# First products that begin as the input arrives, shifted copies by DMA, and a third raw m-tile in the second block

## The chip, the cores and the metric

The kernel runs on one core of one Trainium2 chip. The metric is the device time of one execution in microseconds, from three runs of the kernel before. A core has a matrix engine (TensorE, PE), a vector engine (VectorE, DVE), an activation engine (ScalarE, ACT), GpSimd (POOL) and SyncE (SP); DMAs are issued from the queues of SP, ACT or POOL.

## What is computed

Two transformer blocks in a row, on one sequence of 512 tokens with 1024 channels, all in fp32. Cut to what the change touches:

```
h  = rmsnorm(x, norm_mix)                      # first block
q, kc, vc, ks, vs, kw, vw, gl = split(h @ w_in)
k_cmp = gelu(windows(kc) + pe_k) @ ck_w1 ...   # windows of 32 tokens, stride 16
v_cmp = gelu(windows(vc) + pe_v) @ cv_w1 ...
...                                            # attention, memory attention, conv ffn
x3 = residual;  x = rmsnorm(x3, final_norm)    # end of the first block
h  = rmsnorm(x, norm_g)                        # second block
u, v, za, ab, ab_gate, zb, g_a, g_b = split(h @ w_in_2 + b_in)
t  = ab * sigmoid(ab_gate)                     # then a causal convolution of 31 taps
y_a = gelu(u) * (ws @ layernorm(gelu(v)) + bs) * silu(za)
...                                            # merged, projected, added to x, gated once more
```

## The kernel before

Activations lie in SBUF with channels on the 128 partitions and the 512 tokens along the free dimension, so x is 8 tiles of 128x512. An fp32 operand is held as a high and a low part; `split` makes the high part on ACT and the low part on DVE. `mm` issues three matmuls (high by high, high by low, low by high), so that one output tile over 1024 input channels (`dense`) is 24 matmuls of 128x512. A weight piece of 128x1024 is fetched by SP into one of three slots `wr`, cast by ACT to a slot `wh`, and subtracted by DVE or POOL into a slot `wl` (`weight`; `share` says how many of four pieces go to POOL). The program order is not the order on the engines: a scheduler places instructions on each engine's queue by what they need and when it expects that, and each queue then runs strictly in its own order. All calls go through one wrapper, so every instruction has line 95, and the trace is read by the names of tiles: `x` tiles, products and temporaries are `a`, PSUM banks `ps`, small columns `s`.

**The beginning** (`nsa`, L289). The tiles of x are fetched alternately by SP and ACT, with the first weight in two halves between them. A loop (L304) scales and splits each x[k] and multiplies it at once into the first product `pk[0]`. The second product follows by `dense` (L598), then eight squares with their adds on POOL (`square_sum`), a third product, the sum over channels (`stat`, a matmul by ones), the fourth product, and a broadcast of the inverse norm `rb` over the partitions. Since rmsnorm's factor is per token, products are made from the unnormalised x and multiplied by `rb` after.

**Shifted copies** (`shifted`, L315). For the compressed keys and values each product tile of two groups is multiplied by `rb`, and then for each group ACT writes a tile whose upper 64 partitions hold the group's 64 channels and whose lower 64 hold the same one token later. `hidden` (L346) adds the position code to strided windows of these tiles (`wf`) and multiplies them by ck_w1 or cv_w1 in four quarters q. `keys` (L445) makes from one product two tiles with the same 64 channels in both halves of the partitions, in high and low part: two casts and two subtractions each. `token_gates` (L330) is a product of 16 matmuls and then a sum of its two halves (`fold`). It stands before `cmp_keys`, which takes a list of four jobs to be done between the quarters.

**The second block** (`block2`, L859). The norm of the first block and that of the second are folded into one factor. While it is worked out (`norms`, `norms_out`, L865 to L885), PE multiplies the raw operand: for the first RAW m-tiles the two products p4 and p3 are multiplied by the factor `R["b"]` after, and from m-tile RAW on the operand is the normalised and split one (`f` and `split` in `norms_out`). There DVE also makes the normalised first-block output in place, `t` times final_norm times `r3b`, which is read again only by the residual late in the block. The convolution is 31 taps a tile on DVE, each a SCALAR_TENSOR_TENSOR into a PSUM bank; `taps(n)` allows n more of them, with counts in TAPS for each stage: the m-loop, the two halves hf of v (four banks each, evicted by DVE, BATCH_NORM_STATS2 on each), the u loop, the mixing loop (`ya`), the loop of w_pa.

## Time and profile before

| what | value |
|---|---|
| time, median of 3 runs | 1464.67 us (1464.51 to 1468.86) |
| profiled execution | 1465.02 us, of which the span is 1463.2 us |
| mean granted TensorE clock | 0.993 of full speed |
| busy PE, DVE, ACT, POOL | 1424.6, 922.6, 659.7, 415.9 us |

The span runs from the first to the last instruction of the core; 1.8 us of the execution lie around it. In the timelines each row gives the start of a run of like instructions, its length, engine, operation, tiles (out<-in), form and count, and in brackets how long the engine had been idle before it and whom it waited for. Matmuls overlap, so the length of a pair is longer than their spacing.

### The profile page before, as it was taken

The page shows a single profiled execution, that of the slowest core. Times are in us where ns is not written, and L with a number is a line of the kernel's source. Part 1 is how long each engine was busy: PE and PEld are TensorE (multiplying, and loading weights), DVE is VectorE, ACT ScalarE, POOL GpSimd, SP SyncE. Part 2 cuts the span into 40 slices and gives each one's busy share as a digit, 9 for nine tenths or more (in the row PEclk, how much of TensorE's full clock was granted, in tenths as well). Part 3 has the DMA queues.
Part 4 walks back from the last instruction along what each step waited for, and adds up shares of the span by engine and source line. Part 5 has one row for each costly group of instructions (what it writes and reads, how often), then busy time and mean ns, then how long its engine had stood idle before and what let it go on. Part 6 is the DMA issues. An engine that isn't in the chain of part 4 may idle for free.

```text
span 1463.2 us, 18587 instructions
## 1 busy us (share of the span) xinstructions
PE 1424.6 (97%) x7106; PEld 1190.2 (81%) x7106; DVE 922.6 (63%) x1417; ACT 659.7 (45%) x1135; POOL 415.9 (28%) x347
## 2 busy tenths in 40 slices
PE   7999999999999999999999998999999999999997
PEld 5787878888888888888888886888887888888897
DVE  4858898886455455555643227999939774444464
ACT  4857768774344433332323333223244455423452
POOL 4023536542210221111111134443454440011223
PEclk9999999999999999999999999999999999999998
DMA  6242012114222233333323342332232322332331
GB/s 207 74 143 59 30 44 73 45 44 158 87 73 86 87 101 91 97 101 100 89 92 105 94 126 87 100 90 85 86 87 72 99 76 85 115 101 87 101 101 58
DMA packets 41384, 132.99 MB, mean 91 GB/s; under 512 B 5200, under 2 KB 7504, under 8 KB 41296
## 3 DMA queue, kind: packets, MB, share of 16 engines
q1 hardware_dynamic: 39568, 129.71, 29.4%
q10 hardware_dynamic: 1728, 2.10, 0.4%
q8 instruction: 56, 0.92, 0.3%
q14 instruction: 32, 0.26, 0.1%
HBM read 129.70 MB, written 2.10 MB: 90 GB/s over the span
## 4 chain that ended last, share of the span: by engine, by line
PE 87%; DVE 7%; ACT 2%; issue 1%; POOL 1%; DMA 1%; POOLq 0%; SPq 0%; ACTq 0%
PE ps L95 87%; DVE a L95 5%; ACT a L95 1%; POOL a L95 1%; DVE wl L95 1%; DVE ps L95 1%; ACT wh L95 1%; DMA a<-in_x_dram 1%; POOL wl L95 0%; DMA a<-in_mem_dram 0%; POOL s L95 0%; DVE s L95 0%; POOLq L1272 0%; SPq L95 0%; DVE wh L95 0%
## 5 line engine op out<-in xcount | busy, mean ns | idle before, releaser
L95 PE MATMUL ps<-a,wh 128*128 128x512 f32 (+1 forms) x3136 | 960.7, 388 | 6.8 <-ACT a L95 4.1
L95 PEld LDWEIGHTS ps<-a,wh 128*128 128x128 f32 x3136 | 584.5, 189 | 125.0 <-ACT a L95 5.3
L95 PE MATMUL ps<-a,wl 128*128 128x512 f32 (+1 forms) x1560 | 604.3, 387 | 2.5 <-POOL wl L95 2.4
L95 ACT CAST wh<-wr 128x1024 fp32r<-128x1024 f32 (+1 forms) x225 | 234.8, 1045 | 521.1 <-PE ps L95 319.3
L95 PEld LDWEIGHTS ps<-a,wl 128*128 128x128 f32 x1560 | 294.4, 189 | 61.8 <-POOL wl L95 3.9
L95 DVE TENSOR_TENSOR a<-ps,a 128x512 f32<-128x512 f32 (+5 forms) x284 | 169.9, 614 | 251.5 <-PE ps L95 197.0
L95 POOL TENSOR_TENSOR a<-a,a 128x512 f32<-128x512 f32 (+1 forms) x106 | 137.8, 1304 | 585.5 <-ACT a L95 470.0
L95 DVE TENSOR_TENSOR wl<-wr,wh 128x1024 fp32r<-128x1024 f32 x169 | 219.2, 1298 | 124.5 <-ACT wh L95 123.1
L95 PE MATMUL ps<-a,a 128*128 128x256 f32 (+4 forms) x1180 | 209.0, 321 | 8.3 <-ACT a L95 8.3
L95 POOL TENSOR_TENSOR wl<-wr,wh 128x1024 fp32r<-128x1024 f32 x56 | 134.1, 2395 | 176.6 <-ACT wh L95 167.8
L95 PEld LDWEIGHTS ps<-a,a 128*128 128x128 f32 x1180 | 165.2, 192 | 20.6 <-ACT a L95 10.7
L95 DVE SCALAR_TENSOR_TENSOR ps<-a,vecs,ps 128x483 f32<-128x483 f32 (+24 forms) x240 | 170.3, 735 | 4.5
L95 POOL TENSOR_TENSOR a<-a,s 128x512 f32<-128x512 f32 (+3 forms) x140 | 115.3, 852 | 184.4 <-DVE s L95 106.6
L95 DVE TENSOR_TENSOR a<-a,a 128x512 fp32r<-128x512 f32 (+3 forms) x172 | 120.8, 708 | 38.4 <-ACT a L95 23.9
L95 ACT CAST a<-a 128x512 fp32r<-128x512 f32 (+1 forms) x124 | 76.4, 622 | 77.9 <-DVE a L95 60.2
L95 ACT ACTIVATE a<-a 128x512 f32<-128x512 f32 (+1 forms) x114 | 61.6, 551 | 94.1 <-DVE a L95 93.9
L95 PE MATMUL ps<-wh,a 128*128 128x512 f32 (+1 forms) x320 | 93.6, 373 | 2.6 <-ACT wh L95 2.6
L95 ACT ACTIVATE a<-ps,s 128x256 f32<-128x256 f32 (+4 forms) x148 | 77.4, 528 | 27.3 <-DVE s L95 23.3
L95 DVE SCALAR_TENSOR_TENSOR a<-a,vecs,a 128x511 f32<-128x511 f32 (+3 forms) x92 | 73.3, 801 | 7.1 <-ACT a L95 6.2
L95 ACT CAST a<-ps 128x384 fp32r<-128x384 f32 (+2 forms) x132 | 62.9, 488 | 32.7 <-PE ps L95 27.4
L95 PEld LDWEIGHTS ps<-wh,a 128*128 128x128 f32 x320 | 58.8, 192 | 12.8 <-ACT wh L95 3.0
L95 DVE TENSOR_REDUCE s<-ps 128x1 f32<-128x128 f32 (+4 forms) x136 | 62.0, 490 | 5.1 <-PE ps L95 4.3
(80 smaller groups left out, 675.5 us busy)
## 6 DMA issues: line engine op xcount, KB each, us to landing
wr<-in_w_in_dram SPq DMA_DIRECT2D x56, 512.0 KB, 3.6
wr<-in_ffn_gate_dram SPq DMA_DIRECT2D x22, 512.0 KB, 3.6
wr<-in_ffn_val_dram SPq DMA_DIRECT2D x22, 512.0 KB, 3.5
wr<-in_ffn_d_dram SPq DMA_DIRECT2D x16, 512.0 KB, 3.5
wr<-in_nsa_w_in_dram SPq DMA_DIRECT2D x15, 512.0 KB, 3.6
wr<-in_ca_wk_dram SPq DMA_DIRECT2D x8, 512.0 KB, 3.6
wr<-in_ca_wv_dram SPq DMA_DIRECT2D x8, 512.0 KB, 3.6
wr<-in_nsa_w_out_dram SPq DMA_DIRECT2D x8, 512.0 KB, 3.6
```

Of the source, the lines that this page charges most:

```text
L95: return lambda *a, **k: f(*[_raw(x) for x in a], **{n: _raw(x) for n, x in k.items()})
```

## The change

The two first products begin together: two weights come in halves between the tiles of x, the loop multiplies each x[k] into both, and squares are taken inside it, added by DVE and POOL in turn. A small Square is issued before the first scaling. `shifted` multiplies by `rb` in half-height pieces straight into the two half tiles and fills the other halves by DMAs from POOL's queue, and `keys` copies halves in the same way. The gates' product moves into the list of jobs between the quarters of the compressed keys, as does its sum (`gates_turned`). In the second block RAW is 3, the normalised first-block output is a function `norm_x` that is called tile by tile, five times in the m-loop and three times in the first half of v, and the counts of taps are new: none for m-tiles 0 to 2, then 9 each, 5 in v, 6 with u, 4 in the mixing loop except its last turn, 10 with w_pa.

```diff
@@ -39,3 +39,3 @@
 
-TAPS = (4, 5, 5, 4, 10, 7)
+TAPS = (9, 5, 6, 4, 10)
 
@@ -45,3 +45,3 @@
 SHARE = (4, 0)
-RAW = 2
+RAW = 3
 DEBUG = False
@@ -290,11 +290,14 @@
         nc, I = self.nc, self.I
-        x, raws = [], []
-        w0 = self.wraw.tile([P, 1024], F32)
-        for k in range(KD):
-            x.append(self.a())
-            (nc.scalar if k % 2 else nc.sync).dma_start(x[k], I["x"][k])
-            if k in (0, 2):
-                nc.sync.dma_start(w0[:, 256 * k:256 * k + 512], I["nsa_w_in"][8][:, 256 * k:256 * k + 512])
-            if k in (4, 7):
-                raws.append(self.load(I["nsa_w_in"][9 + len(raws)]))
+        x, xs = [self.a() for _ in range(KD)], []
+        w0 = [self.wraw.tile([P, 1024], F32) for _ in range(2)]
+        for k in (0, 1, 3):
+            nc.scalar.dma_start(x[k], I["x"][k])
+        for c, ks in ((slice(0, S), (2, 4)), (slice(S, 2 * S), (5, 6, 7))):
+            for i in range(2):
+                nc.sync.dma_start(w0[i][:, c], I["nsa_w_in"][8 + i][:, c])
+            for k in ks:
+                nc.sync.dma_start(x[k], I["x"][k])
+        pre = self.sm(1)
+        nc.scalar.activation(pre, self.neghalf[:, 0:1], AF.Square)
+        raw = self.load(I["nsa_w_in"][10])
         nc.sync.dma_start(self.vecs[:, _FIRST:], I["vecs"][:, _FIRST:])
@@ -303,3 +306,13 @@
 
-        xs, w, pk = [], [], [self.ps()]
+        acc = []
+
+        def square(k):
+            sq = self.a()
+            nc.scalar.activation(sq, x[k], AF.Square)
+            if k < 2:
+                acc.append(sq)
+            else:
+                (nc.vector if k % 2 else nc.gpsimd).tensor_tensor(acc[k % 2], acc[k % 2], sq, op=ALU.add)
+
+        pk = [self.ps(), self.ps()]
         for k in range(KD):
@@ -307,5 +320,8 @@
             if k % 4 == 0:
-                w.append(self.split(w0[:, k * P:k * P + S]))
+                w = [self.split(t[:, k * P:k * P + S]) for t in w0]
             s = slice(k % 4 * P, k % 4 * P + P)
-            self.mm(pk[0], (w[k // 4][0][:, s], w[k // 4][1][:, s]), xs[k], k == 0, k == KD - 1)
+            for j in range(2):
+                self.mm(pk[j], (w[j][0][:, s], w[j][1][:, s]), xs[k], k == 0, k == KD - 1)
+            if k >= 2:
+                square(k - 2)
         del w, w0
@@ -317,11 +333,12 @@
             c2 = []
+            L, H = slice(0, 64), slice(64, 128)
             for u in range(2):
-                f = self.a()
-                nc.vector.tensor_tensor(f, p[u], rb, op=ALU.mult)
-                for v in range(2):
-                    s = slice(v * 64, v * 64 + 64)
-                    t = self.a()
-                    nc.scalar.copy(t[0:64], f[s])
-                    nc.scalar.copy(t[64:128, 0:S - 1], f[s, 1:S])
-                    c2.append(t)
+                t, q = self.a(), self.a()
+                nc.vector.tensor_tensor(t[L], p[u][L], rb[L], op=ALU.mult)
+                nc.gpsimd.dma_start(t[H, 0:S - 1], t[L, 1:S])
+                nc.vector.tensor_tensor(q[H, 0:S - 1], p[u][H, 1:S], rb[H, 1:S], op=ALU.mult)
+                nc.vector.tensor_tensor(q[L, 0:1], p[u][H, 0:1], rb[H, 0:1], op=ALU.mult)
+                nc.gpsimd.dma_start(q[L, 1:S], q[H, 0:S - 1])
+                c2.extend((t, q))
+                del t, q
             p.clear()
@@ -329,2 +346,4 @@
 
+        pfs = []
+
         def token_gates():
@@ -338,3 +357,6 @@
                     nc.tensor.matmul(pf, w[:, k], xs[k][j], start=(k == 0 and j == 0), stop=(k == KD - 1 and j == 1))
-            f = self.to_sbuf(pf)
+            pfs.append(self.to_sbuf(pf))
+
+        def gates_turned():
+            f = pfs.pop()
             p = self.ps((P, NT, 48))
@@ -451,6 +473,8 @@
                 h, l = self.a(dt=F32R), self.a(dt=F32R)
-                for o in (u, 1 - u):
-                    so = slice(o * 64, o * 64 + 64)
-                    nc.scalar.copy(h[so], f[s])
-                    nc.vector.tensor_sub(l[so], f[s], h[s].bitcast(F32))
+                so = slice(64 - u * 64, 128 - u * 64)
+                nc.scalar.copy(h[s], f[s])
+                nc.vector.tensor_sub(l[s], f[s], h[s].bitcast(F32))
+                for t in (h, l):
+                    nc.gpsimd.dma_start(t[so].bitcast(F32), t[s].bitcast(F32))
+                del t
                 K[b, 2 * pair + u] = (h, l)
@@ -597,7 +621,12 @@
 
-        pk.append(self.dense([I["nsa_w_in"][9]], xs, raw=raws.pop(0)))
-        acc = []
+        w = self.weight(I["nsa_w_in"][10], raw)
+        del raw
+        square(KD - 2)
+        square(KD - 1)
+        nc.vector.tensor_tensor(acc[0], acc[0], acc.pop(), op=ALU.add)
+        px = [self.ps()]
         for k in range(KD):
-            self.square_sum(x[k], acc)
-        px = [self.dense([I["nsa_w_in"][10]], xs, raw=raws.pop(0))]
+            s = slice(k * P, (k + 1) * P)
+            self.mm(px[0], (w[0][:, s], w[1][:, s]), xs[k], k == 0, k == KD - 1)
+        del w
         x.clear()
@@ -610,4 +639,2 @@
         queries(0)
-        token_gates()
-        wg = None
 
@@ -641,3 +668,4 @@
 
-        cmp_keys(ck, [lambda: keys(1, 0), lambda: queries(1), lambda: None, lambda: None])
+        cmp_keys(ck, [lambda: keys(1, 0), lambda: queries(1), token_gates, gates_turned])
+        del wg
         ck.clear()
@@ -884,3 +912,8 @@
                 R["s"].append(self.split(f))
-                nc.vector.scalar_tensor_tensor(t, t, self.vec("final_norm", k), r3b, op0=ALU.mult, op1=ALU.mult)
+            R["3"] = r3b
+
+        def norm_x(k):
+
+            t = R["x"][k]
+            nc.vector.scalar_tensor_tensor(t, t, self.vec("final_norm", k), R["3"], op0=ALU.mult, op1=ALU.mult)
 
@@ -966,3 +999,5 @@
             del s, t
-            taps(TAPS[0] if m < 2 else TAPS[5])
+            if m >= RAW:
+                taps(TAPS[0])
+                norm_x(m - RAW)
 
@@ -990,2 +1025,6 @@
                 taps(TAPS[1])
+                if hf == 0 and q < RAW:
+                    norm_x(KD - RAW + q)
+                    if q == RAW - 1:
+                        del R["3"]
             for i in range(NT):
@@ -1047,3 +1086,4 @@
             del f, p, t
-            taps(TAPS[3])
+            if m < KD - 1:
+                taps(TAPS[3])
         vt.clear()
```

On DVE, after the first broadcast: a_321 (before) and a_328 (now) are `rb`, ps the products of the compressed keys and values, a_474, a_446 and the like the tiles `wf`, wh_439 the weight of the gates. Before:

```order
L95 TENSOR_TENSOR wh_439<-a_116,wh_439 128x8x64
L95 TENSOR_TENSOR a_323<-ps_118,a_321 128x512
L95 TENSOR_TENSOR a_331<-ps_196,a_321 128x512
L95 TENSOR_TENSOR a_384<-ps_248,a_321 128x512
L95 TENSOR_TENSOR a_392<-ps_285,a_321 128x512
L95 TENSOR_TENSOR a_474<-a_325,vecs 128x4x31
L95 TENSOR_TENSOR a_547<-a_325,vecs 128x4x31
L95 TENSOR_TENSOR a_474<-a_328,vecs 128x4x31
L95 TENSOR_TENSOR a_547<-a_328,vecs 128x4x31
L95 TENSOR_TENSOR a_614<-a_325,vecs 128x4x31
```

and now:

```order
L95 TENSOR_TENSOR a_338<-ps_122,a_328 64x1
L95 TENSOR_TENSOR a_389<-ps_259,a_328 64x512
L95 TENSOR_TENSOR a_390<-ps_259,a_328 64x511
L95 TENSOR_TENSOR a_375<-ps_344,a_328 128x512
L95 TENSOR_TENSOR a_390<-ps_259,a_328 64x1
L95 TENSOR_TENSOR a_396<-ps_292,a_328 64x512
L95 TENSOR_TENSOR a_397<-ps_292,a_328 64x511
L95 TENSOR_TENSOR a_378<-a_375,a_377 64x512
L95 TENSOR_TENSOR a_384<-a_375,a_383 64x512
L95 TENSOR_TENSOR a_397<-ps_292,a_328 64x1
L95 TENSOR_TENSOR a_446<-a_330,vecs 128x4x31
L95 TENSOR_TENSOR a_446<-a_331,vecs 128x4x31
```

Four whole multiplications became eight of half height and four of one column (the last of them stand here); the multiplication and the subtractions of the first key now stand ahead of the first additions of the position code.

On POOL, the same place, now; before, nothing stood between the square root `rt` and the memset for the values:

```order
L95 TENSOR_TENSOR rt<-s_289,neghalf 128x4
L95 DMA a_330<-a_330 64x511
L95 DMA a_331<-a_331 64x511
L95 DMA a_337<-a_337 64x511
L95 DMA a_338<-a_338 64x511
L95 DMA a_389<-a_389 64x511
L95 DMA a_390<-a_390 64x511
L95 DMA a_377<-a_377 64x512
L95 DMA a_383<-a_383 64x512
L95 DMA a_378<-a_378 64x512
L95 DMA a_384<-a_384 64x512
L95 DMA a_396<-a_396 64x511
```

The copies inside a tile are in POOL's queue, those of the compressed keys first, then two of the values', then the key's.

On DVE in the second block, where the operand is normalised: g is the gain, a_8121 (a_8124 now) the factor `R["b"]`, a_8128 (a_8131) `r3b`. Before:

```order
L95 SCALAR_TENSOR_TENSOR a_8165<-a_7825,g_7255,a_8121 128x512
L95 SCALAR_TENSOR_TENSOR a_7728<-a_7728,vecs,a_8128 128x512
L95 TENSOR_TENSOR a_8161<-a_8158,a_8160 128x512
L95 TENSOR_TENSOR a_8168<-a_8165,a_8167 128x512
L95 SCALAR_TENSOR_TENSOR a_7825<-a_7825,vecs,a_8128 128x512
L95 SCALAR_TENSOR_TENSOR a_8172<-a_7922,g_7255,a_8121 128x512
L95 SCALAR_TENSOR_TENSOR a_8179<-a_8019,g_7255,a_8121 128x512
L95 SCALAR_TENSOR_TENSOR a_7922<-a_7922,vecs,a_8128 128x512
L95 TENSOR_TENSOR a_8175<-a_8172,a_8174 128x512
L95 TENSOR_TENSOR a_8182<-a_8179,a_8181 128x512
L95 SCALAR_TENSOR_TENSOR a_8019<-a_8019,vecs,a_8128 128x512
L95 TENSOR_TENSOR ps_8031<-ps_8031,a_8121 128x512
```

and now:

```order
L95 TENSOR_TENSOR a_8166<-a_8163,a_8165 128x512
L95 TENSOR_TENSOR a_8172<-a_8169,a_8171 128x512
L95 SCALAR_TENSOR_TENSOR a_8175<-a_8022,g_7258,a_8124 128x512
L95 TENSOR_TENSOR ps_8034<-ps_8034,a_8124 128x512
L95 TENSOR_TENSOR ps_8088<-ps_8088,a_8124 128x512
L95 TENSOR_TENSOR a_8178<-a_8175,a_8177 128x512
L95 TENSOR_TENSOR ps_8187<-ps_8187,a_8124 128x512
L95 TENSOR_TENSOR ps_8218<-ps_8218,a_8124 128x512
L95 SCALAR_TENSOR_TENSOR a_8184<-ps_8088,vecs,a_8183 128x512
L95 SCALAR_TENSOR_TENSOR a_8252<-ps_8218,vecs,a_8251 128x512
L95 TENSOR_SCALAR ps_8389<-a_8184,vecs 128x512
L95 SCALAR_TENSOR_TENSOR a_7345<-a_7345,vecs,a_8131 128x512
```

The rows with a_8128 (final_norm) are gone from between the normalised tiles and their subtractions; they now stand one by one between taps, the first behind the first tap.

## Rows read from the trace of the kernel before

**Rows 1.** page, the chain that ended last, shares of the span by engine

```profile
PE 87%; DVE 7%; ACT 2%; issue 1%; POOL 1%; DMA 1%; POOLq 0%; SPq 0%; ACTq 0%
```

**Rows 2.** waits of PE; columns: what for, us in total, times, longest

```profile
PE ps L95 <- ACT a L95: 13.7, 7, 7.5
```

**Rows 3.** PE timeline, second block: start, us, what, count [idle before <-releaser]

```profile
888.33 0.70 PE L95 MATMUL ps<-a,wh 128*128 128x512 f32 x2
...
899.33 0.62 PE L95 MATMUL ps<-a,wh 128*128 128x512 f32 x2
...
908.14 0.49 PE L95 MATMUL ps<-a,wh 128*128 128x512 f32 x1 [3.26 <-ACT a L95]
...
911.71 0.93 PE L95 MATMUL ps<-a,wh 128*128 128x512 f32 x2
...
1128.50 0.50 PE L95 MATMUL ps<-a,wl 128*128 128x512 f32 x1 [1.76 <-POOL wl L95]
```

**Rows 4.** timeline of PE, 0 to 80 us

```profile
7.47 7.74 PE L95 MATMUL ps<-a,a 128*128 128x512 f32 x24 [7.47 <-ACT a L95]
...
20.66 0.61 PE L95 MATMUL ps<-a,wh 128*128 128x512 f32 x2
...
27.49 1.15 PE L95 MATMUL ps<-ones,a 128*128 128x1 f32 x8 [1.24 <-POOL a L95]
28.50 1.20 PE L95 MATMUL ps<-a,wh 128*128 128x512 f32 x2
...
35.58 0.60 PE L95 MATMUL ps<-ident,rt 128*128 128x128 f32 x4
...
53.28 0.38 PE L95 MATMUL ps<-wh,a 128*128 128x256 f32 x1 [2.56 <-ACT wh L95]
...
78.67 0.50 PE L95 MATMUL ps<-wl,a 128*128 128x512 f32 x1 [1.32 <-DVE wl L95]
```

**Rows 5.** windows: us, busy PE, PEld, DVE, ACT, POOL, PE clock, DMA

```profile
36.84:78.67 41.83, 37.10 (x179) 31.15 (x177) 37.52 (x69) 34.50 (x53) 3.18 (x5) 0.92 0.29 89
889.12:992.30 103.18, 98.37 (x425) 80.27 (x424) 94.62 (x133) 31.88 (x39) 42.70 (x18) 0.98 0.30 90
```

**Rows 6.** timeline of ACT and its queue, 0 to 20 us

```profile
0.73 1.87 ACTq L95 DMA_DIRECT2D a<-in_x_dram  x4
4.89 1.28 ACT L95 ACT_TABLE_LOAD   x1 [4.89 <-DMA a<-in_x_dram]
...
7.32 2.80 ACT L95 ACTIVATE a<-a,vecs 128x512 fp32r<-128x512 f32 x4
...
13.55 4.27 ACT L95 ACTIVATE a<-a 128x512 f32<-128x512 f32 x8
```

**Rows 7.** ACT groups by form, 36 to 58 us: busy us, mean ns

```profile
L95 ACT COPY a<-a 64x512 f32<-64x512 f32 x8 | 5.0, 620 | 0.9 <-DVE a L95 0.8
...
L95 ACT CAST wh<-wr 128x1024 fp32r<-128x1024 f32 x3 | 3.0, 1044 | 0.0
```

**Rows 8.** DVE groups by form, 36 to 79 us

```profile
L95 DVE TENSOR_TENSOR a<-a,a 64x512 fp32r<-64x512 f32 x12 | 8.9, 740 | 0.2
...
L95 DVE TENSOR_TENSOR a<-ps,a 128x512 f32<-128x512 f32 x6 | 3.8, 683 | 1.5 <-PE ps L95 1.5
```

**Rows 9.** DMA issues; queue, count, KB each, median us from issue to landing

```profile
out_dram<-a ACTq DMA_DIRECT2D x8, 128.0 KB, 2.0
```

**Rows 10.** timeline of DVE, second block

```profile
897.32 2.88 DVE L95 SCALAR_TENSOR_TENSOR a<-a,vecs,a 128x512 f32<-128x512 f32 x1
...
909.88 0.74 DVE L95 SCALAR_TENSOR_TENSOR a<-a,vecs,a 128x512 f32<-128x512 f32 x1
910.54 2.48 DVE L95 TENSOR_TENSOR ps<-ps,a 128x512 f32<-128x512 f32 x4
...
1068.18 0.75 DVE L95 SCALAR_TENSOR_TENSOR a<-ps,vecs,a 128x512 f32<-128x512 f32 x1 [10.29 <-PE ps L95]
```

**Rows 11.** timeline of POOL, second block

```profile
897.27 2.39 POOL L95 TENSOR_TENSOR wl<-wr,wh 128x1024 fp32r<-128x1024 f32 x1 [6.20 <-ACT wh L95]
```

## The prediction

> **What bounds the kernel now.** I read the page's chain of work that ended last first: TensorE (PE) holds 87% of it [rows 1]. So the kernel is as long as its matmuls, plus the places where PE waits or runs at its lower clock, and only those places can give time back. Second, PE's waits: the largest entry is 13.7 us for ScalarE (ACT) in seven waits, one of them 7.5 us, which is the wait for the first data [rows 2]. Third, the timeline of PE. Two products of 24 matmuls each run from 888.33 to 899.33 us, so one undisturbed product takes 5.50 us, 0.229 us a matmul [rows 3]; every stretch below is held against that. Three places stand out.
>
> First, the beginning. The first product starts at 7.47 us. PE then waits 1.24 us for the sum of squares at 27.49, and the product that begins at 28.50 ends only at 35.58: 7.1 us instead of 5.5. The records there show the pair of matmuls at 1.20 us where the pair at 20.66 took 0.61, which is 1.2 GHz after a wait and 2.4 GHz without one [rows 4]. Second, the compressed keys: PE waits 2.56 us at 53.28, and again 1.32 us at 78.67 [rows 4]. Between 36.84 and 78.67 the mean granted clock is 0.92, and VectorE (DVE) is busy 37.52 of 41.83 us, so it and not PE sets the pace there [rows 5]. Third, the second block: the product that starts at 899.33 is done at 911.71, 12.4 us instead of 5.5, with 3.26 us in one wait [rows 3].
>
> **The change, part by part: the beginning.** The activation table is loaded at 4.89 us for 1.28 us, after the input has come, and the first scaling stands behind it [rows 6]. The early Square moves the load ahead of the arrival, so PE starts near 6.2. The two first products now take turns, 48 matmuls or 11.0 us, so PE alone would end at 17.2. ACT has to feed them: 8 scalings at 0.70, 4 half casts at 0.62 and 6 squares at 0.53 make 11.3 us from 4.9 on [rows 6, 7], after which the last k needs a subtraction and six matmuls, some 2.1 us: 18.3. I take 18.0; today the second product ends at 20.66, so 2.7 us are won [rows 4]. The adds of squares are now shared by GpSimd (POOL) and DVE and should be done about 20. One whole product (to 23.5) stands ahead of the sum, so the wait of 1.24 us goes, and with it the 1.6 us of lower clock. Sum, product and broadcast follow at about 24.5, 30.0 and 30.3: the broadcast comes 5.6 us earlier than 35.58.
>
> **The shifted copies.** Removed are 16 ACT copies of half height, 5.0 us for eight of 512 columns [rows 7] and as much for the eight of 511; they keep ACT from casting weights, and the wait at 53.28 is for such a cast. For the four first keys' operands DVE now does 8 half-height multiplications instead of 4 whole ones. Half height is no cheaper by the rows (half-height subtraction 0.74, full-height operation 0.68 [rows 8]), so this adds 4 x 0.68 = 2.7 us to DVE. The keys lose two of four subtractions each; two keys lie in this stretch, 4 x 0.74 = 3.0 us less. DVE's work stays at 37.2 us. It starts later than the 5.6 us suggest, because the copy of the broadcast now stands behind a weight's cast on ACT that itself waits for the last product: 30.0 + 1.04 + 0.6 [rows 7] + a little = 32.0, against 36.84. DVE so ends this stretch at 69.2 if its waits all vanish, and at 73.5 if it waits 4.3 us as now [rows 5]. PE's bound lies lower: its 37.10 us at clock 0.92 are 34.1 at full clock, plus 1.3 from 35.58 to 36.84, which from 30.0 gives 65.4, with one microsecond of stall 66.4. I take 70.7 instead of 78.67: **8.0 us**, between 5.2 (73.5) and 11 (near PE's bound).
>
> **The DMAs on POOL's queue.** The trace has no DMA issued by POOL, so their price is bounded. The first four must land before DVE reaches its first pe additions: 32.0 + 8 x 0.68 + 0.3 for the one-column pieces + 0.68 + 2 x 0.74 for the key, about 39.9. Cheap end: ACT's queue issued four input loads in 1.87 us, 0.47 each [rows 6], and its 128 KB stores land 2.0 us after issue, the size of a half tile here [rows 9]. The last source is ready at about 34.8, so all land by 37.3: hidden by 2.6 us. Dear end: each holds POOL's queue for as long as such a landing takes, 2.0 from 32.7 on, and lands 2.0 later: 42.7, 2.8 us late. I take 0.5 us, nearer to the cheap end, since in the rows issue is the short part and landing the long one. An end below nothing I exclude here, since what the copies freed is counted above. What is behind them on POOL's queue in this stretch is only memsets and casts for values used much later. The Trainium skill ("DMA: Bandwidth & Descriptors", section "Anatomy of one DMA — SWDGE (gpsimd) path") fits about 2.0 us plus bytes/436e3 for one DMA of this queue, mostly completion; that would be an estimate of 2.3 us for 131 KB, and no row here shows it. With it as latency the sum stays; as time in series on the queue the early gain would be about 4.
>
> In the attention loop two more keys lose two subtractions and two casts each and get four DMAs each, ahead of POOL's softmax scalings. PE is busy without a break in most of that loop, so I take nothing, and 1.5 us either way. The gates' product moves from before the compressed keys into them; PE's count of work is the same, and it now fills a place where PE had to wait. Together the first part gives 8.0 - 0.5 = **7.5 us** (4 to 11).
>
> **The second block.** With three m-tiles on the raw operand, PE has two more products, 11 us, before it needs the normalised one. The wait at 899.33 to 911.71 costs 12.4 - 5.5 = 6.9 us and goes. What is late next? DVE still forms the operand: its chain ends at 910.54 today [rows 10], with eight final-norm operations among it, 0.74 each, more where POOL's weight subtraction (2.39 at 897.27) runs at the same time: 2.88 at 897.32 [rows 10, 11]. Without them the chain ends about 904 to 906, then ACT's last casts, table load, two sigmoids and the weight cast for m-tile 3, and POOL's subtraction of 2.4: about 910, and PE wants that weight at 910.2. Margin nearly none; I charge 0.3. The final-norm operations do not vanish; they lie between taps for m-tiles 3 to 7 and in the first half of v, eight at 0.74, plus two multiplications for the third raw tile, 1.3, less the two taps that are put off. From 889.12 to 992.30 DVE is busy 94.62 of 103.18 us [rows 5]: its work ends near 984 to 986.5, while PE, 6.9 us earlier, has v's first half done near 985. PE's next half needs the fourth bank back four matmul groups later, so 0 to 3 us may be lost; I charge 0.7. On the way to the mixing loop DVE has 10.29 us of idle time at 1068.18 [rows 10], enough to take in what is put off. The waits at the loop's end (1.76 us at 1128.50 for POOL's lo half and the ones ahead of it [rows 3]) stay, because the last rows there keep their order. That makes 6.9 - 0.3 - 0.7 = **5.9 us** (2 to 7).
>
> **Sum.** The profiled execution took 1465.02 us, close to the median 1464.67. 1465.0 - 7.5 - 5.9 = 1451.6, which on the scale of the median is 1451.3; I say 1451.5. The measurement separates about 0.3%, 4.4 us, from no change.
>
> **The rivals.** (1) Early gain halved. DVE and POOL get in each other's way: in the second block a DVE operation of 0.74 took 2.88 while POOL's of 2.39 ran [rows 10, 11]. The square adds now run on both, interleaved with the splits that PE waits for. If three POOL adds each hold DVE for half of that loss of 2.1 us, the first products end at 21 instead of 18, and DVE's waits return: gain 4 instead of 7.5, **1455**. The Trainium skill ("SBUF — State Buffer", section "SBUF: two separate sides") says that one of the two blocks for the whole instruction when DVE reads two SBUF inputs; the rows agree, with those 2.1 us. Against it: the adds spread over the arrival of x, where DVE has slack.
>
> (2) The second block gives its gain back: DVE, with the same work and 7 us less time, is late at v's evictions by up to 3 us and again in the mixing loop, where its lag is already the wait at the end. Half to all of 5.9 lost: **1455 to 1457.5**. For it: 94.62 of 103 us busy. Against it: the 10.29 us of idle time.
>
> (3) The change does not do what it says: the first products stay bound by x's arrival and m-tile 3 waits where m-tile 2 did, about **1462**.
>
> (4) Slower: each DMA holds POOL's queue. At 2.0 us each [rows 9] the start loses 2.8 us beyond its cover, and in the loop eight of them hold the softmax scalings queued behind, 16 us uncovered: 2.8 + 16 - 13.9 = 4.9 us longer, **1470**. With nothing covered it decides from about 1.6 us a DMA. For it: nothing in the trace shows what an issue costs POOL, and PE's line of products in the loop waits for what POOL scales. Against it: POOL is idle for most of this stretch and of the loop, so most would be covered.
>
> **How the numbers follow.** Forecast, 1446 to 1454.5: 0.55. Rival 1: 0.16. Rival 2: 0.14. Both at once or rival 3, within 0.3%: 0.09. Rival 4: 0.06. So faster 0.85, same 0.09, slower 0.06. The range takes in the forecast's bounds (8.0 to 11 early, 7 late: 1446) and rivals 1 and 2 (1457.5, with 1.5 for the loop's keys): 1445 to 1459.
>
> **What would show it.** Right: PE begins near 6.2, the broadcast stands at 30 and not at 35.6, no wait above 1 us where the compressed keys begin, PE's wait for the values' weight near 70; in the second block an unbroken run of products from 888 to 910 on the old time scale, and the mixing loop's last waits about 13 us earlier than now. Wrong: a DVE wait for a DMA before its first pe additions (price of POOL's issue), a PE wait for a freed bank between v's halves, POOL rows in the loop that wait for their own queue, or DVE operations of two inputs at two to three microseconds during the first 20.

## The result and the profile after

| | before | changed |
|---|---|---|
| median | 1464.91 us (4 runs, 1464.51 to 1468.86) | 1448.81 us (4 runs, 1447.93 to 1449.44) |
| span of the profiled execution | 1463.2 us | 1447.6 us |
| mean granted clock | 0.993 | 0.995 |

The ratio is 0.9884 with a 95% interval of 0.9865 to 0.9902: 16.1 us faster, where 13.4 were forecast. The time lies inside the stated range. The two halves of the sum do not fit as well: in the profiled execution the first part of the kernel gave 4.4 us (forecast 7.5, from 4 to 11), the second block 11.2 (forecast 5.9, with 7 as its upper bound). One half was 3.1 us short and the other 5.3 over. That the sum comes out near is in part luck, and most of what follows is about the two errors.

The page of the changed kernel first, the chain that ended last, as [rows 1]:

```profile
PE 92%; DVE 4%; ACT 2%; issue 1%; POOL 1%; DMA 1%; SPq 0%; POOLq 0%; ACTq 0%; DVEq 0%
```

PE's share of the chain rose from 87% to 92%; what left the chain is DVE, from 7% to 4%.

PE's timeline of the changed kernel, start, length, what, and in brackets the idle time before it; it answers [rows 4] and [rows 3]:

```profile
5.83 1.65 PE L95 MATMUL ps<-a,a 128*128 128x512 f32 x3 [5.83 <-ACT a L95]
8.11 13.02 PE L95 MATMUL ps<-a,a 128*128 128x512 f32 x45 [0.63 <-ACT a L95]
...
26.41 0.94 PE L95 MATMUL ps<-ones,a 128*128 128x1 f32 x8
...
32.80 0.60 PE L95 MATMUL ps<-ident,rt 128*128 128x128 f32 x4
...
45.54 0.38 PE L95 MATMUL ps<-wh,a 128*128 128x256 f32 x1 [1.23 <-ACT a L95]
...
68.76 1.94 PE L95 MATMUL ps<-fold,a 128*128 128x48 f32 x8 [2.54 <-ACT a L95]
...
875.59 2.11 PE L95 MATMUL ps<-ones,a 128*128 128x1 f32 x16
...
1113.21 0.50 PE L95 MATMUL ps<-a,wl 128*128 128x512 f32 x1 [1.44 <-POOL wl L95]
```

Setting equal places of PE's work side by side, counted in matmuls from the end, gives the lead of the changed kernel, place by place. The broadcast stands at 32.80 instead of 35.58: 2.8 us. At the sum of the second block (875.59; the kernel before has it at 880.00) the lead is 4.4. After the third m-tile it is 11.6 (the 2630th matmul from the end, at 900.84, was at 912.48). In the loop of u it grows to 12.6; there the kernel before has this wait, and the changed one has none:

```profile
1061.97 0.50 PE L95 MATMUL ps<-a,wl 128*128 128x512 f32 x1 [0.68 <-POOL wl L95]
```

At the weight that ended the mixing loop's waits, 1113.21 against 1128.50, it is 15.3, and it stays between 15.3 and 15.6 to the end. So nothing was given back behind the mixing loop, and the gain came in four pieces: 4.4, 7.3, 1.0 and 3.0.

### The profile page after: what moved, and what is told of

Read it like the earlier page. It is cut to its first block, busy times and chain, and to the rows that moved or that the text cites. A ratio compares the mean times of both kernels' runs of the same rounds, so it can differ in the third digit from the quotient of the medians.

```text
span 1447.6 us, 18643 instructions
## 1 busy us (share of the span) xinstructions
PE 1419.3 (98%) x7106; PEld 1189.5 (82%) x7106; DVE 917.0 (63%) x1424; ACT 646.5 (45%) x1113; POOL 418.8 (29%) x367
## 4 chain that ended last, share of the span: by engine, by line
PE 92%; DVE 4%; ACT 2%; issue 1%; POOL 1%; DMA 1%; SPq 0%; POOLq 0%; ACTq 0%; DVEq 0%
PE ps L95 92%; DVE a L95 3%; ACT a L95 1%; DVE wl L95 1%; ACT wh L95 1%; DMA wr<-in_nsa_w_in_dram 0%; POOL a L95 0%; DMA a<-in_mem_dram 0%; POOL s L95 0%; POOL wl L95 0%; DVE s L95 0%; SPq L95 0%; POOLq L1312 0%; DVE wh L95 0%; ACTq L95 0%
## 5 line engine op out<-in xcount | busy, mean ns | idle before, releaser
L95 PE MATMUL ps<-a,wh 128*128 128x512 f32 (+1 forms) x3120 | 950.4, 386 | 0.0
L95 DVE TENSOR_TENSOR a<-ps,a 128x512 f32<-128x512 f32 (+6 forms) x292 | 173.9, 610 | 266.8 <-PE ps L95 212.3
L95 POOL TENSOR_TENSOR a<-a,a 128x512 f32<-128x512 f32 (+1 forms) x102 | 130.3, 1282 | 578.6 <-ACT a L95 463.4
L95 PE MATMUL ps<-a,a 128*128 128x256 f32 (+4 forms) x1204 | 215.9, 324 | 7.4 <-ACT a L95 7.3
L95 PEld LDWEIGHTS ps<-a,a 128*128 128x128 f32 x1204 | 170.8, 192 | 21.2 <-ACT a L95 10.6
L95 DVE SCALAR_TENSOR_TENSOR ps<-a,vecs,ps 128x501 f32<-128x501 f32 (+25 forms) x240 | 167.7, 739 | 3.2
L95 DVE TENSOR_TENSOR a<-a,a 128x512 fp32r<-128x512 f32 (+3 forms) x168 | 115.0, 690 | 35.9 <-ACT a L95 25.1
L95 ACT CAST a<-a 128x512 fp32r<-128x512 f32 (+1 forms) x116 | 71.9, 623 | 82.6 <-DVE a L95 68.2
```

The source lines that it names most:

```text
L95: return lambda *a, **k: f(*[_raw(x) for x in a], **{n: _raw(x) for n, x in k.items()})
```

## The experiments: the first 80 us

The comparisons by time below have intervals of about 0.2% to either side, some 2.5 us, and cannot part variants that differ by one or two. So each is also read by its lead over the kernel before at three places: the broadcast (35.58 before), the sum of the second block (880.00 before), and the end. Ten kernels that share the changed beginning to the letter have their broadcast anywhere from 31.3 to 33.3 us, by when the first half of the second weight lands (its cast starts between 6.60 and 8.00); that scatter is taken out by looking at the lead from the broadcast to 880.00. A second scatter stays in: spells at half clock. Four of the kernels have the same instructions in the same order on every engine up to 870 us, and still differ:

| kernel | cast of the second weight | broadcast | mean granted clock, 66 to 76 us | lead at 880.00 | of it from the broadcast on |
|---|---|---|---|---|---|
| changed | 7.43 | 32.80 | 0.66 | 4.4 | 1.6 |
| `e7_taps5` | 7.42 | 32.91 | 0.66 | 4.6 | 1.9 |
| `e5_raw2` | 6.85 | 31.85 | 1.00 | 7.1 | 3.3 |
| `e6_norm` | 6.79 | 31.65 | 1.00 | 7.3 | 3.4 |

Each kernel has one trace, so differences in lead below 1.8 us prove little unless the clocks are alike.

### Where the lead after 70 us goes: the place of the gates' sum

In the changed kernel PE waits 2.54 us for the sum of the gates' halves at 68.76, and its granted clock is 0.5 for some time after. Its lead over the kernel before falls there from about 9 to about 4.5 us. The first theory was that the sum stands in a bad place: ACT's copy for it is queued behind a cast that waits for DVE.

`e1_gates_first` puts the gates' product one job earlier:

```diff
-cmp_keys(ck, [lambda: keys(1, 0), lambda: queries(1), token_gates, gates_turned])
+cmp_keys(ck, [lambda: keys(1, 0), token_gates, lambda: queries(1), gates_turned])
```

> The changed kernel with the gates' product one slot earlier among the jobs between the quarters of the compressed keys (ahead of the second queries product instead of behind it). Changed kernel: PE waits 2.54 us for the gates' sum at 68.76 and runs at half clock to about 75; its lead over the kernel before falls there from 9.6 to 5.0 us. Theory A (place of the sum: its copy stands on ACT behind a cast that waits for DVE): the copy now stands ahead of that cast, the wait and the half clock go, 3 to 4.6 us are won, about 1444.5 to 1446. Rival B (DVE's chain: the low part of the values' first weight is ready at 71.4 whatever PE does before): PE waits there instead, 1448 to 1449, with a wait for DVE wl of 2 to 3 us near 69.

Measured: 1449.08 us, ratio 0.9885 (0.9870 to 0.9899), the same as the changed kernel. The wait is gone, and two others stand in its place:

```profile
68.70 0.50 PE L95 MATMUL ps<-wl,a 128*128 128x512 f32 x1 [1.25 <-DVE wl L95]
...
72.46 0.69 PE L95 MATMUL ps<-ident,a 128*128 128x128 f32 x2 [2.33 <-ACT a L95]
```

These are rows of PE in `e1_gates_first`: first the low part of the values' weight, made by DVE, then the gelu of the compressed keys, made by ACT. The lead from the broadcast to 880.00 grows by 2.0 us, in the changed kernel by 1.6. Theory A fell; of rival B the place came true, the wait for the low part being 1.25 us instead of 2 to 3. `e1b_gates_before` undoes that part of the change (product and sum ahead of the compressed keys, as in the kernel before):

> The changed kernel with product and sum of the gates back ahead of the compressed keys, where the kernel before has them. Theory A (place of the sum): no wait for the sum near 68, PE's 1.23 us wait at the first quarter is covered by 16 matmuls: about 1444 to 1446. Rival B (DVE's chain sets the end of this stretch): 1448 to 1450, the wait moves to the low part of a weight.

Measured: 1449.32 us, ratio 0.9888 (0.9873 to 0.9903). PE waits 2.37 us for the sum, now at 51.73, then 0.94 and 0.55 us for weights' low parts. The lead grows by 1.0 us. `e8_gates_late` moves product, sum and sigmoids behind the compressed keys:

```diff
-cmp_keys(ck, [lambda: keys(1, 0), lambda: queries(1), token_gates, gates_turned])
+cmp_keys(ck, [lambda: keys(1, 0), lambda: queries(1), lambda: None, lambda: None])
...
             values(q)
+            if q == 0:
+                token_gates()
+                gates_turned()
```

> The changed kernel with product, sum and sigmoid of the gates moved behind the compressed keys, into the first job of the compressed values. So far: moving the product alone (e1_gates_first) took the 2.54 us wait away, but PE then waited 1.25 us for a weight's low part and 2.33 us for the gelu of the compressed keys, ahead of which ACT had two table loads and the gates' sigmoids. Theory A2 (the sigmoids and their two table loads, some 3.4 us of ACT, hold up the gelu and the transposes after it): the gelu comes right after the last quarter, no wait above 1.3 us from 60 to 90, and 2 to 4 us are won: 1445 to 1447. Rival B2 (DVE's chain from the broadcast to about 71 sets the end of the stretch in any order): within 1 us of the changed kernel, 1448 to 1449.5.

Measured: 1451.98 us, ratio 0.9898 (0.9880 to 0.9917), slower than either expectation; the lead grows by 0.3 us only. PE waits 0.88 us for a low part, 0.58 for a weight's cast and 0.96 for the gelu. Three places for the gates, three sets of waits, and no gain in any: what the place of the gates decides is where PE waits, not how long the stretch is.

### What does set the stretch: DVE

The window of the changed kernel from DVE's first multiplication to the end of its last subtraction there (columns as in [rows 5]: length, busy PE, PEld, DVE, ACT, POOL, clock):

```profile
35.00:71.41 36.41, 32.64 (x166) 27.74 (x165) 35.73 (x71) 17.40 (x24) 10.18 (x19) 0.96 0.58 159
```

DVE is busy 35.73 of 36.41 us; ACT is busy for half of it. In `e6_norm`, where the clock held, PE takes the values' first weight as soon as DVE is done with its low part:

```profile
70.72 0.50 PE L95 MATMUL ps<-wl,a 128*128 128x512 f32 x1 [0.28 <-DVE wl L95]
```

`e10_no_lo` tests DVE's part by leaving out eight subtractions on DVE: the low parts of ck_w1 and cv_w1 are not computed, and the high part stands in for them, with as many matmuls.

```diff
-                w = self.weight(I["c%s_w1" % key][q])
+                raw = self.load(I["c%s_w1" % key][q])
+                hi = self.whi.tile([P, 1024], F32R)
+                nc.scalar.copy(hi, raw)
+                w = (hi, hi)
...
```

> The changed kernel without the low parts of the eight weight pieces ck_w1 and cv_w1: the high part is used in their place, so eight subtractions of 1.22 us on DVE are left out, and the matmuls are as many as before. Theory B2 (from the broadcast to 71 us DVE sets the pace: busy 35.7 of 36.4 us): the stretch ends 3 to 6 us earlier, 1443 to 1446. Rival J (the pace is set by the arrival of weights, by ACT or by PE's own waits): less than 1.5 us, 1447.5 to 1449.

Measured: 1445.06 us, ratio 0.9850 (0.9827 to 0.9873), inside what theory B2 expected. The lead from the broadcast to 880.00 grows by 5.4 us instead of 1.6, and the wait for the sum shrinks from 2.54 to 0.53 us (PE in `e10_no_lo`):

```profile
65.92 1.09 PE L95 MATMUL ps<-fold,a 128*128 128x48 f32 x8 [0.53 <-ACT a L95]
```

So DVE sets the pace, and the wait for the sum was one way in which that showed. Not all of the difference in lead is DVE's. The clock from 66 to 76 us is 1.00 here, and the two kernels of the table that have it too gain 3.3 and 3.4, so that 2.0 us are left for the subtractions. Five of the eight stand in this stretch, 6.1 us of DVE's work. They bring less than their length because others bind next: DVE now waits 0.83 and 0.74 us for ACT, and PE 1.36 us at 68.56.

`e4_keys` gives DVE work back: the keys' halves are again made by ACT and DVE.

```diff
-                so = slice(64 - u * 64, 128 - u * 64)
-                nc.scalar.copy(h[s], f[s])
-                nc.vector.tensor_sub(l[s], f[s], h[s].bitcast(F32))
-                for t in (h, l):
-                    nc.gpsimd.dma_start(t[so].bitcast(F32), t[s].bitcast(F32))
-                del t
+                for o in (u, 1 - u):
+                    so = slice(o * 64, o * 64 + 64)
+                    nc.scalar.copy(h[so], f[s])
+                    nc.vector.tensor_sub(l[so], f[s], h[s].bitcast(F32))
```

> The changed kernel with the two halves of the keys' tiles made by ACT and DVE as before instead of by DMAs from POOL's queue. Four keys: two in the stretch that ends at 71, two in the attention loop. Theory B2 (DVE sets the pace before 71): four subtractions more there, 2.8 us, all of it lost; nothing in the loop, where PE is busy throughout: 1450 to 1452. Rival L (the DMAs on POOL's queue cost the loop what they save before it): 1448 to 1449.5, and PE's lead no longer shrinks by 1 us between 210 and 300 us.

Measured: 1449.91 us, ratio 0.9885 (0.9858 to 0.9911); by time alone, B2 and L cannot be told apart. By the lead they can. From the broadcast to 880.00 it grows by 0.4 us (1.6 to 3.4 in the four kernels of the table), and PE waits 2.47 us for a low part at 45.72 and 1.19 at 71.92: DVE's four extra subtractions are paid before 71, some 1.2 to 2.9 us of them. In the loop rival L does not hold. Between 180 and 220 us the changed kernel has PE's matmuls in another order than the kernel before, so that a lead read there, as in the expectation, says nothing. On either side of it the order is the same, and the lead of the changed kernel is 4.5 at 100 us and 4.5 at 300, that of `e4_keys` 5.1 and 4.8. The DMAs of the loop's two keys cost nothing that shows, as forecast.

### The copies and the DMAs

The DMAs on POOL's queue in the changed kernel, first the queue's rows (start, time on the queue, count), then issue to landing (count, KB each, us):

```profile
35.98 1.25 POOL L95 DMA_DIRECT2D a<-a  x2 [6.39 <-DVE a L95]
37.58 0.52 POOL L95 DMA_DIRECT2D a<-a  x1 [0.35 <-DVE a L95]
38.30 0.52 POOL L95 DMA_DIRECT2D a<-a  x1 [0.20 <-issue]
```

```profile
a<-a POOLq DMA_DIRECT2D x16, 128.0 KB, 5.4
...
a<-a POOLq DMA_DIRECT2D x8, 127.8 KB, 2.5
```

An issue holds POOL for 0.52 us (the cheap end said 0.47), and the shifted copies land 2.5 us after it (2.0 there). The Trainium skill's fit of about 2.0 us plus bytes/436e3, 2.3 us here by an estimate ("DMA: Bandwidth & Descriptors", "Anatomy of one DMA — SWDGE (gpsimd) path"), is close to these 2.5; the halves of the keys take longer, 5.4 us in the median, and are in no hurry. The fourth shifted copy was issued at 38.30 and DVE's first addition of the position code began at 43.60 with no wait behind it: the DMAs are hidden. `e3_copies` asks what they replaced is worth. In it `shifted` is that of the kernel before (a whole multiplication, and ACT copies both halves); all else is as changed.

```diff
-                t, q = self.a(), self.a()
-                nc.vector.tensor_tensor(t[L], p[u][L], rb[L], op=ALU.mult)
-                nc.gpsimd.dma_start(t[H, 0:S - 1], t[L, 1:S])
...
+                f = self.a()
+                nc.vector.tensor_tensor(f, p[u], rb, op=ALU.mult)
+                for v in range(2):
+                    s = slice(v * 64, v * 64 + 64)
+                    t = self.a()
+                    nc.scalar.copy(t[0:64], f[s])
+                    nc.scalar.copy(t[64:128, 0:S - 1], f[s, 1:S])
...
```

> The changed kernel with the shifted copies made by ACT from a whole product as before (16 copies of half height), all else as changed. Theory E (the copies hold up ACT's casts): PE waits 2 us or more for ACT at the first quarters, with half clock after it, 1450.5 to 1453. Rival F (ACT has room: it is idle 12 of 24 us in that stretch, DVE's chain decides and has 2.7 us less to do): 1447 to 1449.

Measured: 1450.64 us, ratio 0.9897 (0.9883 to 0.9912). PE in `e3_copies`, at the first quarter of the compressed keys:

```profile
46.99 0.58 PE L95 MATMUL ps<-wh,a 128*128 128x256 f32 x1 [3.55 <-ACT a L95]
```

The wait is 3.55 instead of 1.23 us, and half clock follows, as theory E said. But of the 5.2 us that the kernel, counted from the broadcast, falls behind the changed one by 60 us, 4.9 are made good by 76, while the changed kernel waits for the gates' sum and runs at half clock. Net, the copies cost 1 us in lead (0.7 to 880.00 instead of 1.6), up to 2.7 against the two kernels that kept the clock, and 1.8 by the medians. A wait of 3.5 us ahead of a bound that comes later anyway is worth far less than its length.

### The beginning

`e9_oldstart` undoes the beginning alone (arrival, products, squares as in the kernel before).

> The changed kernel with the beginning of the kernel before (one product while x arrives, the second after it, squares and their adds on POOL after both). Theory B2 (DVE's chain begins with the broadcast, and all of its delay reaches the end of the stretch): the broadcast comes at 35.6 instead of 32.8, and the kernel is 2 to 3 us slower, 1450.5 to 1452. Rival K (PE's lead from the start is absorbed by the later waits): within 1 us, 1448 to 1449.5.

Measured: 1450.73 us, ratio 0.9889 (0.9866 to 0.9911), in the range of B2. The broadcast is at 35.60, and the lead at 880.00 is 3.0 us, against 4.4 to 7.3 in the four kernels of the table. Its clock from 66 to 76 us is 0.84, between theirs, so the beginning is worth 1.4 us at the least and 4.3 at the most; the medians, 1.9 us apart, do not settle it.

`e2_warm` asks why its first products are so slow. In the changed kernel the two first products take from 5.83 to 20.96, at half clock until about 13.5. In `e2_warm`, 16 matmuls of a constant tile run ahead of them:

```diff
+        pw = self.ps()
+        for _ in range(16):
+            nc.tensor.matmul(pw[:, 0:P], self.ones, self.ones, start=True, stop=True)
+        del pw
```

> The changed kernel with 16 matmuls of a constant tile by itself (128x128, fp32, result unused) ahead of the first product, so that PE works from about 1.2 us on. Changed kernel: PE starts at 5.83, gets 1.2 GHz until about 13.5, and the two first products end at 21.1. Theory C (granted clock: the products are slow because PE was idle before): they end at 18.5 to 19.7, the broadcast comes 1.4 to 2.5 us earlier, time about 1446.5 to 1447.5. Rival D (ACT and DVE feed the splits just in time, the last split ends at 18.3): end at 20.5 or later, time 1448.3 to 1449.

Measured: 1449.24 us, ratio 0.9883 (0.9866 to 0.9899): nearer to rival D. PE in `e2_warm`:

```profile
8.89 6.93 PE L95 MATMUL ps<-a,a 128*128 128x512 f32 x29 [2.00 <-ACT a L95]
16.10 1.66 PE L95 MATMUL ps<-a,a 128*128 128x512 f32 x6 [0.27 <-DVE a L95]
18.41 2.81 PE L95 MATMUL ps<-a,a 128*128 128x512 f32 x11 [0.65 <-DVE a L95]
21.05 0.62 PE L95 MATMUL ps<-a,wh 128*128 128x512 f32 x2
```

The 29 matmuls now take 0.239 us each, full clock, and then PE waits for DVE and ends at 21.05, no earlier than in the changed kernel (20.96). What PE gains in clock it spends waiting, first for a weight, then for the splits. The weight is the second one's first half. This is ACT's cast of it in the changed kernel, and ACT's last scaling of x:

```profile
7.43 0.62 ACT L95 CAST a<-wr 128x512 fp32r<-128x512 f32 x1 [1.66 <-DMA wr<-in_nsa_w_in_dram]
...
15.30 0.71 ACT L95 ACTIVATE a<-a,vecs 128x512 fp32r<-128x512 f32 x1
```

In `e2_warm` this cast starts at 8.22, 0.8 us later, so the two ends are not to be compared as they stand. From the cast to the end it is 12.8 us there and 13.5 in the changed kernel; in the ten kernels without the extra matmuls it is 12.8 to 13.7, and the products end at 19.5 to 21.3. So full clock from the start is worth 0.7 us against the changed kernel and nothing against the fastest of the others. DVE's rows of the changed kernel show why they are late, POOL's what stands against them:

```profile
13.78 1.48 DVE L95 SCALAR_TENSOR_TENSOR a<-a,vecs,a 128x512 fp32r<-128x512 f32 x1 [0.23 <-ACT a L95]
...
15.78 1.79 DVE L95 SCALAR_TENSOR_TENSOR a<-a,vecs,a 128x512 fp32r<-128x512 f32 x1
...
17.56 0.74 DVE L95 SCALAR_TENSOR_TENSOR a<-a,vecs,a 128x512 fp32r<-128x512 f32 x1
```

```profile
13.21 1.49 POOL L95 TENSOR_TENSOR a<-a,a 128x512 f32<-128x512 f32 x1 [3.21 <-ACT a L95]
...
15.62 1.40 POOL L95 TENSOR_TENSOR a<-a,a 128x512 f32<-128x512 f32 x1
```

Two splits take 1.48 and 1.79 us while POOL adds squares; the next one, with nothing on POOL beside it, takes 0.74 at 17.56, and the square that DVE adds ahead of it costs another 0.68. This is the mechanism of the first rival, at a little over half the size that was assumed (1.8 us, where three times half of 2.1 were). That the adds of squares hold up the splits is read from the rows; moving them was not tried.

## The experiments: the second block

Two edits act on the wait at the third m-tile: the third raw tile, and the final norm taken out of DVE's chain. `e5_raw2` undoes the first, `e6_norm` the second.

```diff
-RAW = 3
+RAW = 2
```

> The changed kernel with two raw m-tiles instead of three; the final-norm operations still come later. Changed kernel: no wait at the third m-tile, 7.5 us of lead won there. Theory N (taking the final-norm operations out of DVE's chain is most of it): PE waits some 1 to 2.5 us within the third m-tile, 1450 to 1451.5. Theory R (the third raw tile is most of it): waits of 4 us or more and a stretch at half clock, 1453 to 1456.

Measured: 1452.15 us, ratio 0.9899 (0.9884 to 0.9914). In the third m-tile PE has no wait that a row shows, only one pair of matmuls of 0.88 instead of 0.62 us. The lead over the kernel before goes from 5.5 (890) to 12.5 (925): 7.0 of the 7.3 us come without the third raw tile. That is theory N, but for the wait of 1 to 2.5 us that it still expected there. Its range of time missed because of what is lost elsewhere: at 1101.42 PE waits another 1.49 us for POOL, and behind 1200 us the lead loses 1.6 more, 1.02 of it in a wait for POOL at 1211.74. Why POOL is later there stays open.

```diff
                 R["s"].append(self.split(f))
+                nc.vector.scalar_tensor_tensor(t, t, self.vec("final_norm", k), r3b, op0=ALU.mult, op1=ALU.mult)
...
         def norm_x(k):
+            return
...
```

> The changed kernel with the final-norm operations back between the normalised tiles, three raw m-tiles kept. Theory R (the third raw tile is most of it): the operand is there when m-tile 3 wants it, at most 1 us lost there, 1448.5 to 1450. Theory N (DVE's chain then ends 5 us later and the weight of m-tile 3, which stands on ACT behind that chain, with it): PE waits 2 to 5 us at m-tile 3, 1451 to 1455.

Measured: 1447.65 us, ratio 0.9870 (0.9855 to 0.9885). Theory R's picture held here (PE waits nowhere from 880 to 930), and its range of time was a little high. The lead goes from 5.7 (890) to 13.0 (925), 7.3 us, as in the changed kernel, without the final norm being moved. So either edit alone takes away the whole wait, to 0.3 us, and the second adds next to nothing. The forecast priced the wait once, which was right, but it thought the margin nearly none; there was room for eight operations of DVE.

`e11_raw3_alone` is the kernel before with RAW = 3 and no other edit.

> The kernel before with three raw m-tiles and nothing else: final-norm operations between the normalised tiles and the old counts of taps. Kernel before about 1465. So far: either remedy alone, the third raw tile or the final norm moved, leaves less than 1.5 us of the 7.5 us wait. Theory M (each is enough at that place; the rest of the second block's gain comes from what stands on DVE at the end of the mixing loop, which follows the counts of taps): 7 us at the third m-tile, waits at the loop's end as before, 1457 to 1458.5. Rival N2 (the head start alone brings the rest, DVE being earlier): 1454 to 1455.5.

Measured: 1461.67 us (nine runs, 1457.31 to 1462.62), ratio 0.9962 (0.9948 to 0.9977): 5.6 us by the ratio, less than either theory. Of the lead, 7.3 us come at the third m-tile, and 3.5 go again: 1.5 around 916.57, where PE waits 1.20 us for DVE, 0.7 up to the loop of u, where it waits 1.17 us for POOL at 1056.47, and 1.3 at the end of the mixing loop. Its rows of PE there:

```profile
1118.17 0.49 PE L95 MATMUL ps<-a,wh 128*128 128x512 f32 x1 [0.83 <-ACT a L95]
1118.90 0.50 PE L95 MATMUL ps<-a,wh 128*128 128x512 f32 x1 [0.23 <-DVE a L95]
...
1122.99 0.50 PE L95 MATMUL ps<-a,wl 128*128 128x512 f32 x1 [1.75 <-POOL wl L95]
```

These are the waits of the kernel before, to a hundredth (1.76 there [rows 3]). That these 1.3 us were lost is the clock: from 1118 to 1128 us it is 0.83 here and 1.00 in the kernel before. In the changed kernel only the last is left, at 1.44. The difference is in what stands on DVE between the last two mixing products. In `e11_raw3_alone`, as in the kernel before, there are three subtractions that write the split form, one of them blocked for 2.74 us. These are its rows from the blocked one on; the last is the eviction, and the one ahead of it stands at 1106.58:

```profile
1110.50 2.74 DVE L95 TENSOR_TENSOR a<-a,a 128x512 fp32r<-128x512 f32 x1
1113.16 0.72 DVE L95 SCALAR_TENSOR_TENSOR ps<-a,vecs,ps 128x492 f32<-128x492 f32 x1
1113.80 1.14 DVE L95 TENSOR_TENSOR a<-a,a 128x512 fp32r<-128x512 f32 x1
...
1115.50 0.74 DVE L95 SCALAR_TENSOR_TENSOR a<-ps,vecs,a 128x512 f32<-128x512 f32 x1
```

In the changed kernel, whose rows begin with the first of the two evictions, there are two unblocked ones in one run, and the last product is evicted 5.9 us after the one ahead of it instead of 8.9:

```profile
1099.21 0.75 DVE L95 SCALAR_TENSOR_TENSOR a<-ps,vecs,a 128x512 f32<-128x512 f32 x1
...
1101.74 1.29 DVE L95 TENSOR_TENSOR a<-a,a 128x512 fp32r<-128x512 f32 x2
1102.95 2.25 DVE L95 SCALAR_TENSOR_TENSOR ps<-a,vecs,ps 128x488 f32<-128x488 f32 x3
1105.11 0.75 DVE L95 SCALAR_TENSOR_TENSOR a<-ps,vecs,a 128x512 f32<-128x512 f32 x1
```

Is it the new counts of taps that do this, or the earlier start? `e7_taps5` changes one count, the one of the u loop:

```diff
-TAPS = (9, 5, 6, 4, 10)
+TAPS = (9, 5, 5, 4, 10)
```

> The changed kernel with five taps a turn in the loop of u instead of six. In the changed kernel the lag of DVE behind PE at the end of the mixing loop is 5.2 us (8.4 before) and the waits there sum to 1.4 us (3.2 before), which won 2.6 us. Theory G (what matters is what stands on DVE between the last two mixing products; the counts of taps decide that order): with another count the last waits change by 1 us or more either way, 1447 to 1451. Rival H (DVE is simply earlier, by the second block's head start, whatever the counts): the wait at the loop's end stays at 1.4 us, 1448.3 to 1449.3.

Measured: 1453.84 us, ratio 0.9912 (0.9897 to 0.9926): 4.1 us slower than the changed kernel by the two ratios, 4.0 by the lead at the end, further than either expectation. At the end of the mixing loop theory G held, for the better: the last wait, 1.44 us in the changed kernel, is gone. The loss is at a place of which neither spoke. PE in `e7_taps5` at the turn from v's first half to its second:

```profile
986.27 0.59 PE L95 MATMUL ps<-wh,a 128*128 128x512 f32 x1 [2.25 <-DVE a L95]
986.65 0.63 PE L95 MATMUL ps<-wl,a 128*128 128x512 f32 x1
987.08 1.06 PE L95 MATMUL ps<-wh,a 128*128 128x512 f32 x2
```

and DVE there:

```profile
969.95 10.70 DVE L95 SCALAR_TENSOR_TENSOR ps<-a,vecs,ps 128x495 f32<-128x495 f32 x14
981.30 0.81 DVE L95 TENSOR_SCALAR ps<-a,vecs 128x512 f32<-128x512 f32 x1 [0.66 <-ACT a L95]
982.15 1.54 DVE L95 SCALAR_TENSOR_TENSOR ps<-a,vecs,ps 128x511 f32<-128x511 f32 x2
983.73 2.48 DVE L95 TENSOR_TENSOR a<-ps,a 128x512 f32<-128x512 f32 x4
```

Three rows of a new tile's taps, the first of which waits for ACT, stand ahead of the four evictions, and PE waits for a freed bank and then runs at half clock; the lead falls by 4.2 us. In the changed kernel the evictions come straight after the taps, at 980.85:

```profile
969.34 11.48 DVE L95 SCALAR_TENSOR_TENSOR ps<-a,vecs,ps 128x496 f32<-128x496 f32 x15
980.85 2.48 DVE L95 TENSOR_TENSOR a<-ps,a 128x512 f32<-128x512 f32 x4
```

This is the second rival, at the place that it named, with the price that it named (half to all of 5.9). With the counts of the changed kernel the three rows stand elsewhere. That a count in a loop 30 us later moves rows here is the scheduler's doing, which places what is ready by its own times; which of its choices it was is not settled. How much the counts are worth together is bounded by two kernels: `e6_norm` and `e11_raw3_alone` both have three raw m-tiles with the final norm among the normalised tiles, and their second blocks gain 11.3 and 3.8 us. They differ there in the counts, but also in their first parts; no run has the new counts alone.

## Why the prediction was right, and where its terms were not

- **First products: 2.7 us forecast, none measured.** They were to end at 18.0 and end at 20.96, where the kernel before has 20.66 (19.5 to 21.3 in the ten kernels with this beginning). ACT's scalings were done at 16.0, as forecast. What failed is the 2.1 us that were to follow: the last split was ready only at 18.3, since POOL's adds and DVE's own square held DVE up, and PE, behind from its start at half clock, took until 20.96. What the beginning does give is the 1.24 us wait and the 1.6 us of lower clock around the sum of squares, both as forecast: broadcast 2.8 us earlier, not 5.6.
- **DVE's stretch: its end forecast at 70.7, measured at 71.41.** DVE starts 3.0 us later than forecast (35.00, not 32.0) and does 35.7 us of work instead of 37.2, with almost no wait. The bound was named rightly, and `e10_no_lo`, `e4_keys` and the three placings of the gates bear it out. The step from there to the lead, that PE follows DVE, holds where the clock held. In `e6_norm` PE takes the values' first weight at 70.72, where the kernel before takes it at 78.67, and its lead at 880.00 is 7.3 us, where 7.5 were forecast. In the profiled execution of the changed kernel PE takes that weight at 73.62, 2.2 us after DVE is done, and the lead is 4.4. The wait for the gates' sum is the same in both, 2.54 us; the half clock behind it is not. The forecast counted the gates' product as a filler and put this wait and its clock at nothing. It was short by a spell of half clock that the same instructions have in some executions and not in others.
- **DMAs: 0.5 us forecast, nothing measured**, 0.52 us of queue and 2.5 us to landing, close to the cheap end. The slower rival, decided from 1.6 us a DMA, is out.
- **The loop's two keys: nothing forecast**, and nothing measured.
- **The third m-tile: 6.9 less 0.3 forecast, 7.3 measured**; the last of the half clock behind the wait was not in the 6.9, and the margin was larger than thought.
- **The rest of the second block: minus 0.7 forecast, plus 4.0 measured.** The step that failed is the sentence that the last waits of the mixing loop stay because the rows there keep their order. They do not keep it: of three subtractions between the last two products two are left, and none of them is blocked. Three of the 4.0 us come there. And the new counts of taps, which the forecast treated as neutral, are not: `e11_raw3_alone`, with the old ones, gives back 3.5 us behind the third m-tile, and `e7_taps5`, with one count changed, ends 4.0 us behind.

No variant is clearly better than the changed kernel: `e6_norm` has the lowest median of the complete ones, 1447.65, with an interval that overlaps.

## What to carry to other kernels

Before pricing a wait, ask which engine is busy throughout the stretch; there, moving the waiting instruction only moved the wait here, and taking work from that engine shortened the stretch, until another bound came. Two edits against one wait do not add, so price the wait once and undo each edit alone to see which is needed. Where a scheduler orders an engine by expected times, a count that looks like tuning can be worth as much as the edit it accompanies: compare the orders around each eviction that another engine waits for, not only around the place that was edited.

## What the runs showed of the hardware

After the same wait the granted clock went different ways. These are the windows from 66 to 76 us of the changed kernel, of `e7_taps5`, of `e5_raw2` and of `e6_norm`, whose instructions up to there are the same; the last but two of the columns is the clock:

```profile
66.00:76.00 10.00, 7.46 (x32) 6.69 (x32) 5.58 (x14) 7.24 (x12) 2.25 (x4) 0.66 0.46 142
```

```profile
66.00:76.00 10.00, 7.46 (x32) 6.72 (x32) 5.55 (x14) 7.11 (x12) 2.18 (x3) 0.66 0.44 138
```

```profile
66.00:76.00 10.00, 7.36 (x42) 5.90 (x43) 7.42 (x17) 8.79 (x14) 2.79 (x4) 1.00 0.36 106
```

```profile
66.00:76.00 10.00, 7.56 (x43) 6.07 (x44) 7.43 (x16) 8.79 (x14) 2.58 (x4) 1.00 0.38 108
```

PE had waited 2.54 to 2.55 us for the sum in all four. In two the clock was then 0.66 in the mean, part of the time at its lower level of 1.2 GHz, in two it stayed at 1.00, which is 2.4 GHz, and PE did 32 matmuls in the ten microseconds in the first two, 42 and 43 in the others. From the broadcast to 880.00 the lead of the first two grows by 1.6 and 1.9 us, that of the others by 3.3 and 3.4. In the last two the clock fell instead around 876 us, at the 16 one-column matmuls of the sum, where the first two kept it: the leads of both shrink there by 1.6 us. So a stretch at half clock is worth one to two microseconds here and can come or stay away with the same instructions, which is as much as most of these variants differ by. The kernel before is no exception: `e11_raw3_alone`, with the same instructions as it up to 870 us, leads it by 2.1 us at 880.00 and by 0.5 at 890. The lead shows where such a spell falls; it does not take it out.
